# Layer 0 of a hybrid decoder step in two token groups, with one group's conv, norm and attention issued between the other group's dense blocks

## The chip, the cores and the metric

The kernel is one program on one core of a Trainium2 chip. The metric is the device time of one execution in microseconds, as the median over runs. The profile names the engines PE (TensorE matmul), PEld (its weight loads), DVE (VectorE), ACT (ScalarE), POOL (GpSimd) and SP (SyncE, which issues nearly all DMAs). All of them run their own instruction streams in program order and wait for each other through semaphores.

## The reference, cut to what matters

One inference step of a two-layer trunk for 1024 prompt tokens and 64 sample tokens (8 sequences of 8), `D_MODEL` 1024, in float32. Layer 0 is this; layer 1 has another mixer and is not touched in substance.

```python
hn = rms_norm(h, norm_mix_g[0])
a_val, a_gate, q, k, v = split(hn @ w_in)             # 5 x 512 columns
a = causal_depthwise_conv(concat([conv_prev, a_val * sigmoid(a_gate)]), conv_w) + conv_b   # 31 taps, 512 channels
a = silu(layer_norm(a, ln_g, ln_b))
# stick-breaking attention, 8 heads x 64, strictly causal; the sample group has 1024 cached keys in pages besides
z = q @ k.T * scale + bias
after = reverse_cumsum(log_sigmoid(-z)) - log_sigmoid(-z)
b = exp(log_sigmoid(z) + after) @ v
h = h + concat([a, b]) @ w_out
h = h + (silu(g) * u) @ w_ffn_out                     # g, u = split(rms_norm(h) @ w_ffn_in), 2816 each
```

## The kernel before, in words

Activations lie transposed, channels on the partitions and all `T` = 1088 tokens along the free dimension: `hb` holds eight chunks of 128 channels. A dense product is made of column blocks. `mm3` multiplies one 128x128 weight block with the tokens three times (high part by high, high by low, low by high part, for float32 accuracy out of the fast `float32r` type), in three PSUM banks of 364, 364 and 360 tokens: 9 matmuls for a weight block, 72 for a "half".

A half is 128 output columns over 8 input chunks (or 2 input chunks by 512 output columns), 512 KB of weights. `w_load` fetches it through SP into `stage`, `w_split` makes the high part on ACT (line 132) and the low part on POOL (line 133). `w_next` runs this a few halves ahead. The layer-0 stream is 20 halves for the input projection, 8 for the output projection and 66 for the channel mixer; layer 1 has 16, 8 and 66. Every half is fetched and split once, for all 1088 tokens.

The order of the work is written out in program order (`manual_schedule`), one stage after another:

- Start: x is loaded and transposed, its norm made; the input projection begins. DVE evacuates each block from PSUM, times the norm (`scaled`, line 200).
- Conv (`conv_ops`): beside the input projection, by a list of work pieces that `bg(9.0)` takes from after each block. DVE does 21 of the 31 taps of a chunk as multiply-adds from SBUF to SBUF (line 491, one instruction for the prompt and one for the sample tokens). ACT and POOL do 10 taps of the first three chunks (lines 498 and 500).
- Sample attention, with the conv branch's layer norm in between: cached keys are transposed on PE (line 770) and split, scores (797), chances multiplied up by a scan on DVE, weights transposed, values multiplied (877, 886). No dense block runs here.
- Prompt attention, 8 heads x 8 blocks of 128 queries, in four pipelined steps `s1` to `s4`: scores (1069) and their sigmoids on ACT, the mask on POOL (1083), the reverse scan and a product on DVE (1084, 1086), the transposed weights (1106, `ring`), the values (1118, 256 queries at once). The next head's operands are made piece by piece on DVE and POOL (1018, 1020). Only at its end do the first products of the output projection appear.
- Output projection (`run_out`) and channel mixer (`run_ffn`): ACT takes the Silu, POOL multiplies gate by value (325), ACT and DVE split the hidden block (155, 156). Its last two halves (`to_mixer`) also make the operands of layer 1: squares on ACT and POOL, low parts on DVE (line 266).

Layer 1 follows with its own mixer and channel mixer; at the end the output rows are transposed and stored.

Of the kernel before, what the change touches and what calls it, by code (L numbers as in the profile page):

```python
# [27 lines left out]
EXT = CW - 1 + SEQ          # prompt part of the conv rows  # L28
SCW = 8 + CW - 1            # rows of one sample sequence
# [6 lines left out]
# the sums of a column block: two banks at once, then the third  # L36
def parts(acc, *flat):
    yield (acc[:, 0:2, :NW],) + tuple(f[:, 0:2 * NW].rearrange("p (b n) -> p b n", b=2) for f in flat)
    yield (acc[:, 2, :T - 2 * NW],) + tuple(f[:, 2 * NW:T] for f in flat)


@with_exitstack
def trunk_kernel(ctx, tc, x_prompt, x_sample, cache_k, cache_v, state_conformer, state_shortconv, state_pool,
# [8 lines left out]
    tmps = ctx.enter_context(tc.tile_pool(name="tmps", bufs=3))  # L52
# [3 lines left out]

    def tmp():
        return tmps.tile([128, 1152], F, name="tmp")

# [39 lines left out]
    # blocks of the even projection: value 0, gate 1, q 2, k 3, v 4  # L99
    EVEN = [(j, c) for c in range(4) for j in (0, 1, 2, 3)] + [(4, c) for c in range(4)]  # L100
    for j, c in EVEN:
        add_in(w_in_even[0], 512 * j + c * 128)
    for n in range(8):
        add_in(w_out_even[0], n * 128)
    add_ffn(0)
    # blocks of the odd projection: gb 0, gc 1, xv 2, u 3
# [9 lines left out]
    wlim = [len(EVEN)]                # halves that may be fetched so far  # L116

    def w_load(upto):
        while nxt[0] < min(upto, wlim[0]):
            i = nxt[0]  # L120
            src, kt = seq[i]
            stage[i] = wpool.tile([128, 1024], F, name="stage", bufs=4)
            sp.dma_start(stage[i].rearrange("p (k n) -> p k n", k=kt), src)
            nxt[0] += 1

    def w_split(upto):
        while nxt[1] < min(upto, wlim[0]):
# [11 lines left out]
    def w_next(live=0):               # live: halves before this one whose products are not issued yet  # L139
        j = wj[0]  # L140
        wj[0] += 1
        w_split(j + 3 - live)
        w_load(j + 7 - live)
        return hls.pop(j)

# [1 line left out]
    def mm3(acc, wh, wl, x, first, last):  # L147
        for s, (w, xi) in enumerate(((wh, 0), (wh, 1), (wl, 0))):
            for b, (c0, c1) in enumerate(BLOCKS):
                pe.matmul(acc[:, b, :c1 - c0], w, x[:, xi, c0:c1],  # L150
                          start=first and s == 0, stop=last and s == 2)
# [9 lines left out]
    def add_squares(src, first):  # L161
        if first:
            act.activation(ss[:, :T], src, AF.Square)
            return
        t = tmp()
        act.activation(t[:, :T], src, AF.Square)  # L166
        pool.tensor_tensor(ss[:, :T], ss[:, :T], t[:, :T], op=OP.add)  # L167
# [11 lines left out]
        # one Newton step behind the table's square root  # L179
# [5 lines left out]
    def norm_a(ps, count):  # L185
        norm_cols(ps, count, 0, 9)
        dg = tmp()
        dve.tensor_tensor(dg.rearrange("p (t n) -> p t n", t=9), ident[:, None, :].to_broadcast([128, 9, 128]),
                          rstd[:, :, None].to_broadcast([128, 9, 128]), op=OP.mult)
        return dg  # L190

    def norm_b(ps, dg):
        for c0, c1 in ((0, 512), (512, 1024), (1024, T)):
            m = ps()
            pe.matmul(m[:, :c1 - c0], ones, dg[:, c0:c1], start=True, stop=True)
            act.activation(rr[:, c0:c1], m[:, :c1 - c0], AF.Copy)

    def scaled(dst, acc):
        for a, d, r in parts(acc, dst, rr):
            dve.tensor_tensor(d, a, r, op=OP.mult)  # L200

    def added(dst, acc):
        for a, d in parts(acc, dst):
# [12 lines left out]
    def block(a, h, x, ks=K0, mid=None):  # L216
        for i, k in enumerate(ks):
            if i == 4 and mid:
                mid()
            mm3(a, h[:, 0, k], h[:, 1, k], x[k], k == ks[0], k == ks[-1])  # L220

    # two column blocks at once, over the k blocks as they come
    def pair_open(accs):
        return (accs(), w_next()), (accs(), w_next(1))

    def pair_k(st, x, ks, k):
        for a, h in st:
            mm3(a, h[:, 0, k], h[:, 1, k], x[k], k == ks[0], k == ks[-1])

    def pair(accs, x, ks, hooks, st=None, done=0):  # L230
        st = st or pair_open(accs)
        for k in ks[done:]:
            pair_k(st, x, ks, k)
# [4 lines left out]
    def run_in(accs, x, evacs, hooks, bg=lambda us: None, ks=K0, tail=(lambda: None,) * 2):  # L238
        a0, a1 = pair(accs, x, K0, hooks)
        evacs[0](a0)  # L240
        evacs[1](a1)
        bg(14.0)
        for i, e in enumerate(evacs[2:]):
# [3 lines left out]
            block(a, h, x, ks if end else K0, flush)  # L247
# [5 lines left out]
            bg(9.0)  # L253
# [4 lines left out]
    def low(n=0):                     # low parts held back so that they do not stand before the next sums  # L258
# [3 lines left out]
    def prep(x, n, g, squares=False):  # L262
        act.activation(x[n][:, 0], hb[:, n], AF.Copy, scale=g)  # L263
        if squares:
            add_squares(hb[:, n], n == 0)
# [1159 lines left out]
```

## Time and profile before

| | |
|---|---|
| median of 3 runs | 2767.51 us (2767.29 to 2769.02) |
| span of the profiled execution | 2767.4 us |
| PE busy | 2593.5 us, 94% of the span |
| DVE busy | 1186.8 us, 43% |
| POOL busy | 981.4 us, 35% |
| ACT busy | 726.7 us, 26% |
| DMA | 171.96 MB, mean 62 GB/s |

The table's busy shares are means over stages that differ much. A busy instruction of DVE or POOL can include time in which it stands still, so a group's mean duration is to be held against the same instruction elsewhere in the trace. The profiled execution's span is its time from the first to the last instruction; its own time is not listed apart, and the span differs from the median of the runs by 0.1 us.

### The profile page before, as it was taken

To read this page: it belongs to the slowest core of one execution; us is meant where nothing else is said; L and a number is where in the kernel's file an instruction comes from. 1 tells how busy PE (TensorE), PEld (TensorE's weight loads), DVE (VectorE), ACT (ScalarE), POOL (GpSimd) and SP (SyncE) were. 2 spreads that over 40 slices of the span, in tenths; PEclk is the share of its full clock that TensorE was granted. 3 is DMA by queue.
4 is the path that set the end of the run, shared out by engine and by line. 5 is a ranking of instruction groups with operands and counts; after the bars stand their busy time and mean duration, and the time that the engine had idled before them with its cause. 6 is when DMAs were issued, how large, how long until landed. Compare 5 with 4: busy or idle time off the path is not lost.

```text
span 2767.4 us, 35971 instructions
## 1 busy us (share of the span) xinstructions
PE 2593.5 (94%) x15167; PEld 2470.7 (89%) x15167; DVE 1186.8 (43%) x1455; ACT 726.7 (26%) x1038; POOL 981.4 (35%) x497
## 2 busy tenths in 40 slices
PE   7967988777899999999999999999999999999997
PEld 7967955455699999999999999999999999999997
DVE  5889876688623222222222263342322222222226
ACT  4332165566522111111111132122211111111112
POOL 5666223387543222222222242224322222222222
PEclk9988999899999999999999999999999999999999
DMA  6111265212211111111111131131111111111101
GB/s 206 34 41 41 76 229 190 61 39 62 79 46 46 44 41 46 46 46 39 46 46 46 40 112 47 39 106 46 46 47 39 46 47 46 39 46 46 46 31 65
DMA packets 201096, 171.96 MB, mean 62 GB/s; under 512 B 7121, under 2 KB 164945, under 8 KB 200472
## 3 DMA queue, kind: packets, MB, share of 16 engines
q1 hardware_dynamic: 200904, 169.66, 19.6%
q8 instruction: 120, 1.97, 0.3%
q14 instruction: 40, 0.33, 0.0%
q10 hardware_dynamic: 32, 0.01, 0.0%
HBM read 147.76 MB, written 18.69 MB: 60 GB/s over the span
## 4 chain that ended last, share of the span: by engine, by line
PE 81%; DVE 11%; POOL 4%; ACT 2%; issue 1%; DMA 0%; POOLq 0%; DVEq 0%; ACTq 0%; SPq 0%
PE acc L150 74%; DVE hb L491 5%; POOL be L1083 1%; POOL qq L1020 1%; PE o L877 1%; POOL kk L1020 1%; DVE be L1086 1%; PE kts L770 1%; DVE x L266 1%; PE z L797 1%; PE blk L1337 1%; PE o L1118 1%; DVE kth L774 1%; PE m L1106 0%; PE m L415 0%
## 5 line engine op out<-in xcount | busy, mean ns | idle before, releaser
L150 PE MATMUL acc<-x,hl 128*128 128x364 f32 (+1 forms) x10080 | 1706.5, 331 | 24.4 <-DVE tmp L200 17.1
L150 PEld LDWEIGHTS acc<-x,hl 128*128 128x128 f32 x10080 | 1688.9, 189 | 29.8 <-DVE tmp L200 17.3
L133 POOL TENSOR_TENSOR hl<-stage,hl 128x1024 fp32r<-128x1024 f32 x181 | 440.1, 2434 | 1292.4 <-ACT hl L132 825.4
L150 PE MATMUL acc<-hid,hl 128*128 128x364 f32 x3024 | 507.7, 329 | 0.9 <-DVE hb L204 0.9
L150 PEld LDWEIGHTS acc<-hid,hl 128*128 128x128 f32 x3024 | 504.1, 188 | 1.6 <-PE acc L150 1.4
L200 DVE TENSOR_TENSOR tmp<-acc,rr 128x728 f32<-128x728 f32 x228 | 154.4, 719 | 806.6 <-PE acc L150 800.2
L204 DVE TENSOR_TENSOR hb<-acc,hb 128x728 f32<-128x728 f32 x368 | 249.3, 719 | 352.8 <-PE acc L150 352.3
L132 ACT ACTIVATE hl<-stage 128x1024 fp32r<-128x1024 f32 x181 | 190.1, 1054 | 747.5 <-issue 384.9
L491 DVE SCALAR_TENSOR_TENSOR hb<-ext,par,hb 128x1024 f32<-128x1024 f32 (+1 forms) x180 | 208.9, 1232 | 0.0
L312 ACT ACTIVATE tmp<-tmp 128x1088 f32<-128x1088 f32 x44 | 49.0, 1113 | 367.9 <-DVE tmp L200 367.9
L167 POOL TENSOR_TENSOR ss<-ss,tmp 128x1088 f32<-128x1088 f32 x31 | 92.9, 2998 | 129.8 <-ACT tmp L166 129.1
L325 POOL TENSOR_TENSOR tmp<-tmp 128x1088 f32<-128x1088 f32 x44 | 111.5, 2535 | 38.3 <-ACT tmp L312 38.3
L156 DVE TENSOR_TENSOR hid<-tmp,hid 128x1088 fp32r<-128x1088 f32 x44 | 56.9, 1292 | 139.6 <-ACT hid L155 139.6
L155 ACT ACTIVATE hid<-tmp 128x1088 fp32r<-128x1088 f32 x44 | 49.1, 1116 | 216.6 <-POOL tmp L325 216.6
L1084 DVE TENSOR_TENSOR_SCAN q<-q,ss 128x1024 f32<-128x1024 f32 (+3 forms) x64 | 105.0, 1640 | 1.7 <-ACT q L1074 1.4
L1106 PE MATMUL m<-ident,be 128*128 128x128 f32 x288 | 48.0, 298 | 54.4 <-DVE be L1086 51.5
L500 POOL TENSOR_TENSOR hb<-hb,tapb 128x1088 f32<-128x1088 f32 x27 | 89.0, 3295 | 25.2 <-ACT tapb L498 23.9
L1106 PEld LDWEIGHTS m<-ident,be 128*128 128x128 f32 x288 | 33.9, 150 | 70.3 <-issue 51.5
L266 DVE SCALAR_TENSOR_TENSOR x<-hb,par,x 128x1088 fp32r<-128x1088 f32 x32 | 71.2, 2233 | 25.0 <-ACT x L263 25.0
L1086 DVE TENSOR_TENSOR be<-be,q 128x1023 f32<-128x1023 f32 (+3 forms) x64 | 58.0, 906 | 34.6 <-POOL be L1083 32.5
L1118 PE MATMUL o<-ring,tmp 128*64 128x256 f32 (+1 forms) x320 | 71.6, 372 | 0.0
L1118 PEld LDWEIGHTS o<-ring,tmp 128*64 128x64 f32 x320 | 42.4, 141 | 28.9 <-issue 8.8
(236 smaller groups left out, 1572.9 us busy)
## 6 DMA issues: line engine op xcount, KB each, us to landing
stage<-in_w_ffn_in_dram SPq DMA_DIRECT2D x88, 512.0 KB
stage<-in_w_ffn_out_dram SPq DMA_DIRECT2D x44, 512.0 KB
stage<-in_cache_k_dram SPq DMA_DIRECT2D x64, 256.0 KB
stage<-in_w_in_even_dram SPq DMA_DIRECT2D x20, 512.0 KB
vst<-in_cache_v_dram SPq DMA_DIRECT2D x40, 256.0 KB
park<-hb SPq DMA_DIRECT2D x16, 544.0 KB
hb<-park SPq DMA_DIRECT2D x16, 544.0 KB
stage<-in_w_in_odd_dram SPq DMA_DIRECT2D x16, 512.0 KB
```

What stands on the lines that cost most here:

```text
L132: act.activation(hl[:, 0], st, AF.Copy)
L133: pool.tensor_tensor(hl[:, 1], st, f32(hl[:, 0]), op=OP.subtract)
L150: pe.matmul(acc[:, b, :c1 - c0], w, x[:, xi, c0:c1], start=first and s == 0, stop=last and s == 2)
L167: pool.tensor_tensor(ss[:, :T], ss[:, :T], t[:, :T], op=OP.add)
L200: dve.tensor_tensor(d, a, r, op=OP.mult)
L204: dve.tensor_tensor(d, a, d, op=OP.add)
L266: lowq.append(lambda: dve.scalar_tensor_tensor(x[n][:, 1], hb[:, n], g, f32(x[n][:, 0]), op0=OP.mult, op1=OP.subtract))
L325: pool.tensor_tensor(t[:, :T], t[:, :T], u[:, :T], op=OP.mult)
L491: dve.scalar_tensor_tensor(o, i, w, o, op0=OP.mult, op1=OP.add)
L500: pool.tensor_tensor(a2[:, :T], a2[:, :T], t[:, :T], op=OP.add)
L1084: dve.tensor_tensor_scan(q[:, :n][:, ::-1], q[:, :n][:, ::-1], late[:, 1024 - n:][:, ::-1], 1.0, op0=OP.mult, op1=OP.max)
L1118: pe.matmul(o[:, c:], vrow[hp][:, j, hh], ring[:, (b + j) % RING, c:], start=j == 0, stop=j == nk - 1)
```

## The change

Layer 0's tokens are cut into two groups: GA has tokens 0 to 511, GB tokens 512 to 1087 (512 prompt and 64 sample tokens). `Grp` gives each its column blocks: GA one bank of 512 columns, GB two of 288; layer 1 keeps 364/364/360 (`GT`). The dense stages of layer 0 run per group: input projection GA, input projection GB, output projection and channel mixer GA, the same for GB. The weight stream therefore holds every layer-0 half twice: 94 more fetches and splits.

Everything else of layer 0 becomes a generator that issues a piece and yields a cost in us. After a dense block, `bg(us)` runs pieces worth that many us. While the last blocks of GA's input projection (from its block 12) and GB's input projection run, the pieces are GA's conv, layer norm and attention; while GA's output projection and channel mixer run, they are GB's conv, layer norm and attention and then the whole sample attention. Nothing is issued between the blocks of GB's channel mixer but the squares of GA for the next norm.

The taps keep their split between engines, now for all four chunks (10 taps on ACT and POOL, 21 on DVE) and for 512 or 512+64 tokens at a time. The prompt attention works on 128 queries at a time throughout; its scan is cut in two (the masked 128 columns, then the rest). The sample attention makes all its value products in full float32, with two value slots in place of eleven. GA's channel mixer takes the sigmoid on ACT and one more product on POOL in place of the Silu. Stage buffers go from 4 to 3.

```diff
-NW = 364           # token block of one PSUM bank; the third has 360
-BLOCKS = [(0, NW), (NW, 2 * NW), (2 * NW, T)]
+GA = Grp(0, HALF, 512)
+GB = Grp(HALF, T, 288)
+GT = Grp(0, T, 364)
...
+    for _ in range(2):
+        for j, c in EVEN:
+            add_in(w_in_even[0], 512 * j + c * 128)
+    for _ in range(2):
+        for n in range(8):
+            add_in(w_out_even[0], n * 128)
+        add_ffn(0)
...
+    def bg(us):
+        owed[0] = min(owed[0] + us, us + 4.0)
+        while flow and owed[0] > 0:
+            try:
+                cost = next(flow[0])
+            except StopIteration:
+                flow.pop(0)
+                continue
+            if cost is None:
+                return
+            owed[0] -= cost
...
+            if sig:
+                s = tmp()
+                act.activation(s[:, :n], t[:, :n], AF.Sigmoid)
+                pool.tensor_tensor(t[:, :n], t[:, :n], s[:, :n], op=OP.mult)
...
+                for j in range(OFF, CW):
+                    w = pc(CONVW + j * 4 + c)
+                    for o, i in io(a, g.c0, j):
...
+                            dve.scalar_tensor_tensor(o, i, w, o, op0=OP.mult, op1=OP.add)
+                    if j % 2 and j // 2 - OFF // 2 < OFF:
+                        otap(j // 2 - OFF // 2)
+                    yield 0.8 if g is GA else 1.07
...
+            for u in range(len(units) + 3):          # attention(g): 8 heads x 4 query blocks
+                if u >= 3:
+                    s4(u - 3)
+                if 2 <= u < len(units) + 2:
+                    s3(u - 2)
+                if 1 <= u < len(units) + 1:
+                    s2(u - 1)
...
+                    s1(u)
+                for _ in range(2):
+                    if small:
+                        small.pop(0)()
+                yield 1.7 if g is GA else 3.6
...
+    def slot_a(i):
...
+        bg(3.2)
+    in_proj(GA, x1a, 2, slot_a)
...
+    def slot_b(i):
+        bg(7.3)
+    in_proj(GB, x1, 0, slot_b)
+    drain()
...
+    def flow_c():
+        yield from conv(GB)
+        yield from conv_norm(GB)
+        yield from attention(GB)
+        kstack.close()
+        yield from sample()
...
+    def slot_c():
+        bg(6.9)
+    run_out(GA, accs, x1, FFNG, slot=slot_c)
...
+    run_ffn(GA, accs, ms, hidp, x1, last_a, sig=True, slot=slot_c)
...
+    run_out(GB, accs, x1, FFNG)
...
+        run_ffn(GB, accs, ms, hidp, x1, to_mixer, slot=slot_d)
```

POOL in the conv. Before, beside the input projection: L133 makes the low part of a weight half, L500 adds a tap, L577 is the gate product.

```order
L577 TENSOR_TENSOR tmp<-tmp 128x1088
L582 MEMSET ext 128x30
L133 TENSOR_TENSOR hl<-stage,hl 128x1024
L500 TENSOR_TENSOR hb<-hb,tapb 128x1088 x2
L133 TENSOR_TENSOR hl<-stage,hl 128x1024
L500 TENSOR_TENSOR hb<-hb,tapb 128x1088 x3
```

Now, POOL in GB's conv beside GA's channel mixer: L153 is the weight half, L670 the tap, L363 and L377 are the two products of the hidden blocks.

```order
L153 TENSOR_TENSOR hl<-stage,hl 128x1024
L377 TENSOR_TENSOR tmp<-tmp 128x512
L363 TENSOR_TENSOR tmp<-tmp 128x512
L670 TENSOR_TENSOR a_4162<-a_4162,tapb 128x576 x3
L153 TENSOR_TENSOR hl<-stage,hl 128x1024
L670 TENSOR_TENSOR a_4162<-a_4162,tapb 128x576 x2
L153 TENSOR_TENSOR hl<-stage,hl 128x1024
L377 TENSOR_TENSOR tmp<-tmp 128x512
L670 TENSOR_TENSOR a_4358<-a_4358,tapb 128x576 x2
```

Between two weight halves still stand two or three taps, but a half is now used for 512 tokens, so POOL gets them in half the dense time, with the hidden blocks' products besides.

PE in the prompt attention. Before: L1106 transposes weights, L1069 makes scores, L1118 multiplies the values, with nothing else around them.

```order
L1106 MATMUL m<-ident,be 128x128 x8
L1069 MATMUL z_5095<-kk,qq 128x256 x2
L1118 MATMUL o_5107<-ring,tmp 64x256 x3
L1118 MATMUL o_5107<-ring,tmp 64x128
L1106 MATMUL m<-ident,be 128x128 x7
L1069 MATMUL z_5124<-kk,qq 128x384 x4
```

Now, GB's attention (L797 values, L788 transposes, L760 scores) and the block of GA's channel mixer that follows (L170, acc).

```order
L788 MATMUL m<-ident,be 128x128 x7
L760 MATMUL z_6334<-kt,qa 128x320
L760 MATMUL z_6334<-kt,qz_4851 128x320
L760 MATMUL z_6334<-kt,qa 128x320
L760 MATMUL z_6334<-kt,qz_4851 128x320
L797 MATMUL o_6343<-wt,vrow 64x128 x7
L788 MATMUL m<-ident,be 128x128 x6
L760 MATMUL z_6367<-kt,qa 128x512
L760 MATMUL z_6367<-kt,qz_4852 128x512
L760 MATMUL z_6367<-kt,qa 128x512
L760 MATMUL z_6367<-kt,qz_4852 128x512
L170 MATMUL acc<-hid,hl 128x512 x24
```

One or two steps of the attention, each of values, transposes and scores, now stand between two dense blocks of 24 matmuls; the transposes of the second step need the product that DVE makes after the first was issued.

More of the change, by code (lines that the diff above doesn't have):

```diff
@@ L142, in w_next, with mm3 @@
         w_split(j + 3 - live)
-        w_load(j + 7 - live)
+        w_load(j + 6 - live)
         return hls.pop(j)
-    def mm3(acc, wh, wl, x, first, last):
+    def mm3(g, acc, wh, wl, x, first, last):
         for s, (w, xi) in enumerate(((wh, 0), (wh, 1), (wl, 0))):
-            for b, (c0, c1) in enumerate(BLOCKS):
+            for b, (c0, c1) in enumerate(g.blocks):
                 pe.matmul(acc[:, b, :c1 - c0], w, x[:, xi, c0:c1],
@@ new lines, in trunk_kernel @@
+    feed(GA, x1a, 0)
+    w_split(2)
+    feed(GA, x1a, 1)
+    feed(GA, x1a, 2)
+    hooks = {c - 3: [lambda c=c: feed(GA, x1a, c)] for c in range(3, KC)}
+    hooks[5] = [rest]
+    a0, a1 = pair(GA, accs, x1a, K0, hooks)
+    raw = [tmp(), tmp()]
+    for a, o in parts(GA, a0, raw[0]):
+        act.activation(o, a, AF.Copy)
+    for a, o in parts(GA, a1, raw[1]):
+        dve.tensor_copy(o, a)
+    for hf in range(2):
+        for t in range(4, 9):
+            load_x(hf, t)
+    attention_constants()
@@ L539, in trunk_kernel @@
[L539 to L556 removed]
+    glu_done = set()
```

1429 lines of the change are left out of this document (663 added, 766 removed).

## The prediction

> **What bounds the kernel now.** I first cut the span into its stages and read every engine's busy time in each. The columns after the stretch are the busy us of PE, PEld, DVE, ACT and POOL, then the granted clock, the DMA share and GB/s.
>
> ```profile
> core 0: us, PE busy (x) PEld busy (x) DVE busy (x) ACT busy (x) POOL busy (x), PEclk, DMA share, GB/s
> 0.00:60.00 60.00, 45.29 (x265) 41.75 (x265) 33.45 (x37) 30.84 (x34) 37.10 (x21) 0.97 0.69 229
> 60.00:340.00 280.00, 234.03 (x1350) 228.99 (x1349) 248.40 (x236) 76.64 (x120) 137.64 (x52) 0.91 0.15 45
> 340.00:528.00 188.00, 154.74 (x740) 99.55 (x740) 123.82 (x215) 102.74 (x223) 56.50 (x26) 0.94 0.54 178
> 528.00:744.00 216.00, 156.33 (x810) 109.87 (x810) 172.16 (x147) 135.70 (x256) 160.94 (x142) 0.92 0.19 47
> 744.00:1610.00 866.00, 865.60 (x5190) 863.35 (x5191) 230.76 (x305) 149.39 (x143) 245.43 (x100) 1.00 0.15 48
> 1610.00:1671.00 61.00, 57.96 (x333) 55.34 (x332) 38.29 (x39) 27.35 (x29) 34.38 (x13) 0.97 0.31 111
> 1671.00:2767.40 1096.40, 1079.49 (x6485) 1071.89 (x6483) 339.96 (x478) 204.04 (x235) 309.39 (x145) 1.00 0.16 49
> ```
>
> From 744 on PE is full. Ahead of it lie start, input projection with conv, sample attention and prompt attention; PE is not full there, and this is what the change wants to fill. So I looked at what bounds the conv stage: the groups by shape in its window 84 to 258 (five DVE and POOL groups, one evacuation), and behind the dots the same kinds of instruction over the whole trace.
>
> ```profile
> L491 DVE SCALAR_TENSOR_TENSOR hb<-ext,par,hb 128x1024 f32<-128x1024 f32 x53 | 87.0, 1642 | 0.0
> L491 DVE SCALAR_TENSOR_TENSOR hb<-ext,par,hb 128x64 f32<-128x64 f32 x52 | 70.6, 1358 | 0.0
> L200 DVE TENSOR_TENSOR tmp<-acc,rr 128x728 f32<-128x728 f32 x4 | 3.6, 904 | 0.0
> L500 POOL TENSOR_TENSOR hb<-hb,tapb 128x1088 f32<-128x1088 f32 x27 | 89.0, 3295 | 25.2 <-ACT tapb L498 23.9
> L133 POOL TENSOR_TENSOR hl<-stage,hl 128x1024 fp32r<-128x1024 f32 x10 | 25.7, 2573 | 0.0
> ...
> L1247 DVE SCALAR_TENSOR_TENSOR hb<-ext,par,hb 128x1024 f32<-128x1024 f32 x8 | 10.2, 1280 | 0.0
> L1247 DVE SCALAR_TENSOR_TENSOR hb<-ext,par,hb 128x64 f32<-128x64 f32 x8 | 2.2, 280 | 0.0
> L1224 POOL TENSOR_TENSOR tmp<-tmp 128x1088 f32<-128x1088 f32 x4 | 10.1, 2531 | 0.0
> L133 POOL TENSOR_TENSOR hl<-stage,hl 128x1024 fp32r<-128x1024 f32 x181 | 440.1, 2434 | 1292.4 <-ACT hl L132 825.4 <-issue 451.2 <-DMA xt<-in_x_prompt_dram 15.8
> L200 DVE TENSOR_TENSOR tmp<-acc,rr 128x728 f32<-128x728 f32 x114 | 104.4, 915 | 806.6 <-PE acc L150 800.2 <-issue 6.1
> L156 DVE TENSOR_TENSOR hid<-tmp,hid 128x1088 fp32r<-128x1088 f32 x44 | 56.9, 1292 | 139.6 <-ACT hid L155 139.6
> ```
>
> The 64-wide tap takes 1358 ns in the conv and 280 in layer 1, the POOL add 3295 against 2531. The evacuation, whose one input is PSUM, takes 904 and 915: it is not slowed. So DVE instructions with both inputs in SBUF and POOL's tensor operations wait for each other, a whole instruction at a time. At their undisturbed durations the work is 53x1.28 + 52x0.28 + 27x2.53 + 10x2.43 + 2x2.53 (gate products) = 180 us, in a window of 174: DVE and POOL together act as one resource, filled 1.03 times over. I call it the pair.
>
> The prompt attention shows the same at the level of single instructions (scan, POOL low part, POOL mask, product, then a scan of 128 and a product of 127).
>
> ```profile
> 578.91 2.29 DVE L1084 TENSOR_TENSOR_SCAN q<-q,ss 128x1024 f32<-128x1024 f32 x1
> 579.02 2.71 POOL L1020 TENSOR_TENSOR kk<-kall,kk 64x256 fp32r<-64x256 f32 x1 [2.93 <-ACT be L1074]
> 581.81 0.45 POOL L1083 TENSOR_TENSOR be<-be,tri 128x128 f32<-128x128 f32 x1
> 582.30 1.22 DVE L1086 TENSOR_TENSOR be<-be,q 128x1023 f32<-128x1023 f32 x1 [1.09 <-POOL be L1083]
> ...
> 565.08 0.41 DVE L1084 TENSOR_TENSOR_SCAN q<-q,ss 128x128 f32<-128x128 f32 x1
> 592.27 0.29 DVE L1086 TENSOR_TENSOR be<-be,q 128x127 f32<-128x127 f32 x1 [1.08 <-POOL be L1083]
> PE m L1106 <- DVE be L1086: 51.5, 38, 3.1
> ```
>
> The low part stands 2.71 us, 2.2 of them behind the scan; then mask; then product: one after the other. The last line is the wait that costs PE most: transposes behind the product, 51.5 us in 38 times.
>
> The Trainium skill says the same in "SBUF — State Buffer", "Who interferes with whom": a VectorE instruction with two SBUF inputs and a GpSimd instruction that reads SBUF exclude each other for the whole instruction, one SBUF input does not contend. The trace agrees (1358 against 280 ns, 904 against 915). By the rule taken strictly nothing overlaps, and the two conv sections below would be 10 us longer; I keep the measured 1.03.
>
> **The change part by part.** Prices of the pair, on straight lines through those rows: POOL 0.17 + 2.17 ns a column (0.45 at 128, 2.53 at 1088), so 1.28 us at 512 and 1.42 at 576; a weight half 2.4; a tap 0.75 at 512 and 0.28 for the sample tokens; a DVE tensor operation 0.69 at 512, 0.76 at 576; a scan 0.41 at 128, then 0.27 for each further 128.
>
> PE's prices come from steady pieces of the chain (a piece, its us, its count):
>
> ```profile
> 866.16 753.11 PE acc L150 x4518
> 2721.59 1.06 PE blk L1337 x6
> 404.99 0.48 PE z L797 x4
> 553.38 2.52 PE o L1118 x12
> 2721.26 0.33 PE m L1354 x3
> ```
>
> Per column these are 0.460 ns (363 wide), 0.460 (384) and 0.455 (264): proportional, no floor seen, so 512 costs 0.235 us and 288 costs 0.132. A half takes 24x0.235 = 5.64 us for GA and 48x0.132 = 6.34 for GB, together 11.98, as 72x0.1667 = 12.0 before. *Dense PE time does not change.* A float32 value product of 256 columns takes two passes of 0.21 us, a transpose 0.11. What changes is who works beside it, and how often weights are split: 94 more halves x 2.4 = 226 us more for the pair, all in layer 0. The second fetch is 94x0.5 MB; the sample stage with 33.5 MB of pages moved 178 GB/s, GA needs 0.52 MB per 5.64 us = 93: hidden.
>
> Section by section (counts of the instructions as they now stand), pair against PE; the longer sets the time:
>
> - Start and first 12 halves of GA. Before, the first products came at 20 us after nine token tiles; now four, I take 15. Then 12x5.64 + 10 of transposes and norm, and 8 for the norm's chain: 101.
> - GA's conv, 15 halves. A chunk: 20 taps x0.75 + 9 adds x1.28 + 0.7 = 27.2; four 109. Weights 36, gate products 5, first sums of the norm 4: pair 154. PE 95. 154/1.03 = 150.
> - GA's norm, 4 halves: PE 27, pair 30, in a chain: 35.
> - GA's attention, 9 halves. A head: masks 4x0.45, scans 3.7, products 2.0, two low parts 2.6: 10.0; eight 80, weights 22, rest of the norm 5: 107. PE 57 + 40 = 97. Both near full, and a step's transposes wait for its product: I add 10 per cent: 118.
> - GB's conv, 19 halves of GA's output projection and mixer. A chunk: 20x(0.75+0.28) + 9x1.42 + 0.8 = 34.2; four 137. Weights 46, squares 9, low parts 6, hidden blocks 12: pair 210 against PE 110. 210/1.03 = 204. *This is the worst place:* a half of 5.64 us waits for about 11 of the pair.
> - GB's norm, 5 halves: pair 43, PE 30: 45.
> - GB's attention, 18 halves. A head: masks 1.8, scans 8.1, products 4.1, low parts 3.8: 17.8; eight 143. Weights 43, hidden blocks 20: 206. PE 18x5.64 + 89 = 191. With 5 per cent for waits: 216.
> - Sample, 30 halves: PE 169 + 130 (72 value products of 0.84 = 60, 292 transposes 32, scores 30, rest 8) = 299; the pair has 123. Transposes turn over in two PSUM buffers; 0.3 us for 48 steps: 314.
> - Last two halves: 12.
> - GB's output projection and mixer: 72x6.34 = 457 + 10 for change of buffers and the norm: 467. The pair has 243 there and nothing to do besides.
>
> To here: 101 + 150 + 35 + 118 + 204 + 45 + 216 + 314 + 12 + 467 = 1662. Before, this point, the start of the mixer's last two halves, was at 1610:
>
> ```profile
> 1599.76 28.58 PE L150 MATMUL acc<-hid,hl 128*128 128x364 f32 x170
> 1664.66 3.04 PE acc L150 x18
> ```
>
> The first row is PE's last long run in layer 0; its last 108 products (18 us) belong to those halves, the other 36 come singly behind it. The second is the end of the next pair of blocks, at 1667.7: 57 us, in which DVE and POOL held PE up. Now the two halves are 11.3 us shorter on PE and the squares smaller: 46. The rest, 1100 us, stays. 1662 + 46 + 1100 = 2808. The overlaps at the seams (up to three evacuation buffers let PE run on into the next section) I put at 8: **2800 us**. The profiled execution's span is 2767.4, the median 2767.5, so nothing has to be added.
>
> What hides the added splits in GB's mixer is PE (243 against 458 us). In GA's sections that cover is gone, which is where the loss arises; the saving is the empty PE time of the old conv and attention stages (46 us of 280, 33 of 188 and 60 of 216 by the busy rows, more at full pace), and the two nearly cancel.
>
> **Rivals.**
> *PE sets the pace everywhere* (faster). If queued work of the pair were caught up in the next section, or the two engines overlapped, the sections would take PE's 101 + 95 + 30 + 97 + 110 + 35 + 191 + 314 + 12 = 985, and the total 2598. For it: over all sections the pair has 948 us and PE 936, so perfect smoothing would nearly do it. Against it: evacuations stand in DVE's order behind the taps, so PE can lead by three blocks only, and the conv rows above. It decides from 38 us below my sum (2762): with no waits in the attentions (-21), seams counted twice (-8) and an overlap of 1.06 (-10). 0.20.
> *Waits inside the steps* (slower still). PE issues in order, so a transposition that waits now holds a dense block. At 1.36 us (51.5/38) for each of 67 attention steps in place of the 21 us above: +70, 2870. For it: the longest wait row; against it: the product is issued a step earlier. 0.12.
> *Sample values late.* Two value slots instead of eleven: if each of 32 page pairs waits 2 us, +64, 2864. For it: the 178 GB/s of that stage; against it: 49 MB in 314 us are 156. 0.08.
>
> **How the numbers follow.** No change I call within 0.2% of 2767.5, about what runs of this kernel can tell. My case 0.54 (2773 to 2850), its edge with no change 0.06, PE's pace 0.20, the two slower rivals 0.20. Faster 0.20, same 0.06, slower 0.74. Range 2735 (no seams lost, waits all hidden) to 2870.
>
> **What the profile will show.** Dense matmuls at the same pace in GB's mixer, PE full there. In GB's conv PE busy about half, taps far above 0.75 us, POOL adds above 1.42. In the sample section PE near full. Layer 1 unchanged to 10 us. It is wrong if GB's conv section takes near 110 us, or if GB's attention or the sample section exceed PE's time by over 30.

## The result, and the profile after

The changed kernel takes 2956.1 us (median of four runs, 2954.9 to 2957.1) against 2767.4 (four runs, 2767.3 to 2769.0): 1.068 times as long, interval 1.0666 to 1.0696. The direction was forecast, the size was not: +189 us instead of +33, outside the range.

The profiled execution has a span of 2955.4 us. Cut at the borders of the forecast's sections, every engine's busy time reads like this (columns as in the prediction's first view):

```profile
core 0: us, PE busy (x) PEld busy (x) DVE busy (x) ACT busy (x) POOL busy (x), PEclk, DMA share, GB/s
0.00:101.00 101.00, 85.62 (x358) 65.30 (x359) 34.76 (x69) 40.82 (x58) 56.52 (x40) 0.97 0.56 170
101.00:243.00 142.00, 109.03 (x597) 95.55 (x595) 129.58 (x109) 53.92 (x78) 102.63 (x57) 0.88 0.27 77
243.00:298.00 55.00, 40.17 (x252) 37.76 (x252) 15.71 (x21) 16.21 (x23) 36.73 (x24) 0.77 0.15 44
298.00:446.00 148.00, 114.67 (x726) 96.36 (x725) 77.50 (x122) 63.98 (x150) 67.19 (x64) 0.90 0.20 54
446.00:661.00 215.00, 130.66 (x502) 100.32 (x500) 175.57 (x211) 81.24 (x152) 126.20 (x67) 0.79 0.21 61
661.00:731.00 70.00, 43.12 (x164) 33.14 (x162) 27.83 (x38) 19.42 (x28) 48.97 (x31) 0.76 0.15 42
731.00:985.00 254.00, 213.62 (x1169) 174.67 (x1168) 162.87 (x163) 120.19 (x191) 138.16 (x92) 0.92 0.17 47
985.00:1329.00 344.00, 315.66 (x1385) 215.90 (x1384) 132.71 (x258) 116.78 (x239) 95.95 (x52) 0.98 0.49 143
1329.00:1343.00 14.00, 11.07 (x47) 8.29 (x45) 13.84 (x16) 5.95 (x9) 5.13 (x3) 1.00 0.79 261
1343.00:1810.00 467.00, 465.13 (x3504) 464.21 (x3505) 127.06 (x172) 123.95 (x148) 223.88 (x109) 1.00 0.29 86
1810.00:1856.00 46.00, 39.54 (x232) 37.87 (x230) 23.39 (x25) 18.56 (x23) 21.85 (x11) 0.89 0.30 100
1856.00:2955.40 1099.40, 1082.45 (x6504) 1074.55 (x6502) 341.49 (x481) 206.25 (x238) 312.54 (x146) 1.00 0.16 50
```

Row by row against the forecast: start 101 (101), GA's conv 142 (150), its norm 55 (35), its attention 148 (118), GB's conv 215 (204), norm 70 (45), attention 254 (216), sample 344 (314), last halves 14 (12); then GB's output projection and mixer 467 (467), the pair of blocks behind it 46 (46), the rest 1099.4 (1100). From GB's projection on, where TensorE is nearly full, everything was forecast to a microsecond. The 101 us of the first row are the forecast's own border and not a measurement: the twelfth half ends at 106.5 us in the trace, and the first tap of GA's conv starts at 115.9, behind the thirteenth half. The miss is +148 us in the interleaved sections: the two convs together have +3, the norms +45, the attentions +68, the sample section +30. The +3 hangs on the border: here TensorE's wait for the norm's sums (9.9 and 17.1 us) counts to the norm; counted to the conv, as in the table of the experiments, GB's conv takes 231.

In GB's conv (stretch 461 to 655) the groups are those foreseen: the 64-wide tap at 885 ns, the POOL add at 1789 where the prediction's straight line gives 1420.

```profile
L678 DVE SCALAR_TENSOR_TENSOR hb<-ext,par,hb 128x512 f32<-128x512 f32 x69 | 78.0, 1130 | 0.0
L678 DVE SCALAR_TENSOR_TENSOR hb<-ext,par,hb 128x64 f32<-128x64 f32 x68 | 60.2, 885 | 0.0
L670 POOL TENSOR_TENSOR a<-a,tapb 128x576 f32<-128x576 f32 x32 | 57.3, 1789 | 9.4 <-ACT tapb L668 6.4 <-issue 1.5
```

TensorE's waits in all interleaved sections, longest first (waiting matmul, releaser, total us, times, longest):

```profile
PE m L656 <- DMA stc<-in_state_conformer_dram: 56.6, 4, 22.3
PE m L788 <- DVE be L778: 30.3, 19, 4.6
PE m L218 <- POOL ss L689: 27.0, 2, 17.1
PE acc L170 <- DVE hb L230: 21.3, 5, 10.2
PE z L760 <- POOL kt L740: 15.6, 2, 9.1
PE acc L170 <- POOL hl L153: 11.7, 4, 4.7
```

The first is a load of conv states that I had not foreseen. The second (transposes behind the product) and third (the norm's matmul of ones behind GpSimd's sums) are waits of a *step* (one round of the norm or the attention) while dense work stands behind it in TensorE's order.

### The profile page after: what moved, and what is told of

The parts are those of the page before. It is cut to its first block, busy times and chain, and to the rows that moved or that the text cites. A ratio compares the mean times of both kernels' runs of the same rounds, so it can differ in the third digit from the quotient of the medians.

```text
span 2955.4 us, 37943 instructions
## 1 busy us (share of the span) xinstructions
PE 2650.7 (90%) x15423; PEld 2403.9 (81%) x15423; DVE 1262.3 (43%) x1679; ACT 867.3 (29%) x1334; POOL 1235.8 (42%) x688
## 5 line engine op out<-in xcount | busy, mean ns | idle before, releaser
L153 POOL TENSOR_TENSOR hl<-stage,hl 128x1024 fp32r<-128x1024 f32 x278 | 679.2, 2445 | 1265.3 <-ACT hl L152 899.4
L170 PE MATMUL acc<-x1t,hl 128*128 128x364 f32 (+1 forms) x4896 | 825.0, 330 | 7.1 <-DVE hb L230 6.5
L170 PEld LDWEIGHTS acc<-x1t,hl 128*128 128x128 f32 x4896 | 818.1, 190 | 9.2 <-ACT x1t L304 6.7
L170 PE MATMUL acc<-x,hl 128*128 128x288 f32 (+1 forms) x4704 | 790.9, 329 | 25.0 <-POOL hl L153 8.8
L170 PEld LDWEIGHTS acc<-x,hl 128*128 128x128 f32 x4704 | 713.8, 193 | 96.1 <-issue 13.6
L170 PE MATMUL acc<-hid,hl 128*128 128x364 f32 (+2 forms) x3024 | 518.8, 331 | 21.3 <-DVE hb L230 21.3
L170 PEld LDWEIGHTS acc<-hid,hl 128*128 128x128 f32 x3024 | 482.7, 190 | 54.4 <-DVE hb L230 24.4
L226 DVE TENSOR_TENSOR tmp<-acc,rr 128x728 f32<-128x728 f32 (+2 forms) x230 | 160.7, 721 | 792.0 <-PE acc L170 786.8
L230 DVE TENSOR_TENSOR hb<-acc,hb 128x728 f32<-128x728 f32 (+2 forms) x368 | 255.6, 720 | 325.3 <-PE acc L170 324.2
L678 DVE SCALAR_TENSOR_TENSOR hb<-ext,par,hb 128x512 f32<-128x512 f32 x240 | 265.9, 1155 | 2.4
L170 PE MATMUL acc<-x1a,hl 128*128 128x512 f32 x480 | 126.8, 420 | 8.3 <-POOL hl L153 7.1
L670 POOL TENSOR_TENSOR a<-a,tapb 128x512 f32<-128x512 f32 (+1 forms) x72 | 123.3, 1712 | 19.4 <-ACT tapb L668 14.5
L377 POOL TENSOR_TENSOR tmp<-tmp 128x512 f32<-128x512 f32 (+2 forms) x66 | 117.1, 1774 | 28.0 <-ACT tmp L365 28.0
L170 PEld LDWEIGHTS acc<-x1a,hl 128*128 128x128 f32 x480 | 93.6, 199 | 33.5 <-POOL hl L153 8.9
L797 PE MATMUL o<-wt,vrow 128*64 128x128 f32 x576 | 79.9, 286 | 10.1 <-ACT wt L789 9.7
L797 PEld LDWEIGHTS o<-wt,vrow 128*64 128x64 f32 x576 | 64.0, 141 | 29.2 <-ACT wt L789 20.9
L788 PE MATMUL m<-ident,be 128*128 128x128 f32 x288 | 50.3, 308 | 30.3 <-DVE be L778 30.3
```

The lines of the kernel that those rows point to most:

```text
L153: pool.tensor_tensor(hl[:, 1], st, f32(hl[:, 0]), op=OP.subtract)
L170: pe.matmul(acc[:, b, :c1 - c0], w, x[:, xi, c0:c1], start=first and s == 0, stop=last and s == 2)
L230: dve.tensor_tensor(d, a, d, op=OP.add)
L377: pool.tensor_tensor(t[:, :n], t[:, :n], u[:, :n], op=OP.mult)
L670: pool.tensor_tensor(a2, a2, t, op=OP.add)
L678: dve.scalar_tensor_tensor(o, i, w, o, op0=OP.mult, op1=OP.add)
```

## The experiments

To compare sections I read their borders from TensorE's timeline: the first matmul of the norm's sums, the first scores, the first 512-wide block of GA's output projection, the first page transpose, the first 288-wide block of GB's output projection. A wait ahead of such a matmul here counts to the section before it, so the changed kernel's row differs a little from the windows above. GA's conv is counted from 101 us in every row. All columns but the last two are spans in us; then the time at which GB's projection begins, and the device time. Dense halves move a little from section to section; the two columns at the right do not care. e10, b1, b2 and b3 are medians of four runs (the runs of one kernel lie up to 7 us apart), the others single runs.

| kernel | GA conv | norm | attention | GB conv | norm | attention | sample, last | GB projection begins | total |
|---|---|---|---|---|---|---|---|---|---|
| changed | 152 | 55 | 140 | 231 | 59 | 255 | 350 | 1343 | 2956.1 |
| e1 states early | 151 | 55 | 142 | 232 | 60 | 255 | 351 | 1345 | 2959.4 |
| e2 no low parts | 126 | 49 | 143 | 193 | 53 | 234 | 347 | 1246 | 2858.3 |
| e4 norm apart | 152 | 51 | 127 | 231 | 74 | 238 | 334 | 1307 | 2919.9 |
| e6 half slots | 154 | 48 | 129 | 230 | 57 | 240 | 329 | 1288 | 2901.5 |
| e7 = e4 + e6 | 154 | 48 | 122 | 232 | 70 | 225 | 314 | 1266 | 2878.2 |
| e5 all DVE | 146 | 47 | 135 | 213 | 54 | 235 | 352 | 1283 | 2896.7 |
| e10 = e7 + e5 | 146 | 45 | 118 | 205 | 64 | 212 | 317 | 1207 | 2823.7 |
| e9 = e7 + e2 | 126 | 43 | 110 | 194 | 59 | 214 | 313 | 1162 | 2773.9 |
| e11 = e9, one tap | 101 | 42 | 110 | 138 | 57 | 214 | 313 | 1075 | 2688.9 |

### Is the longest wait on the path? (e1)

```
 with tc.tile_pool(name=f"conv{g.c0}", bufs=1) as ep:
+    for c in range(4 if g is GB else 0):
+        stcs.append(ep.tile([128, 2, 128], F, name="stc", bufs=4))
+        ...                                    # both loads, as before
...
-        stc = ep.tile([128, 2, 128], F, name="stc")
+        stc = stcs[c]
```

> The changed kernel with the conv states of all four channel chunks of the second group loaded when its conv begins, instead of each with its chunk. In the changed kernel TensorE waits 56.6 us in this section for the state's loads (22.3, 14.4 and 19.5 us at one time). Theory A (the pair of VectorE and GpSimd sets the conv's time, the wait only lies beside it): GB conv stays at 215 us within 10, the total at 2946 to 2956; TensorE waits there for something else. Theory B (the late load is on the path): GB conv falls by about 50, the total to about 2905.

Measured 2959.4: nothing gained. TensorE's waits in that conv (446 to 662) show why:

```profile
PE acc L170 <- DVE hb L230: 23.5, 4, 11.8
PE acc L170 <- POOL hl L153: 19.3, 9, 3.6
PE acc L170 <- DVE tmp L226: 17.4, 2, 12.6
PE acc L170 <- ACT hl L152: 14.2, 4, 6.5
PE m L659 <- DMA stc<-in_state_conformer_dram: 1.5, 1, 1.5
```

The state's wait fell from 56.6 to 1.5 us, and the waits for evacuations (lines 230, 226) and weight splits (153, 152) rose from 26.0 to 74.4. So the load was not what held the conv; that the pair holds it (VectorE's two-input instructions and GpSimd's, which take turns) is what e2 and e11 show. The wait that TensorE's list put first had a cover. A long wait row is a place, not a price.

### Whose work sets which section? (e2)

```
+            if i < 114:
+                hls[i] = High(hl[:, 0]...)     # index for low part gives the high part
+                nxt[1] += 1
+                continue
             pool.tensor_tensor(hl[:, 1], st, f32(hl[:, 0]), op=OP.subtract)
```

> The changed kernel without GpSimd's low parts of the weights for the first 114 halves (all up to GB's output projection): the third product of each matmul triple takes the high part once more, so TensorE, ScalarE and the loads do what they did, and the output lacks the weights' low parts there. GpSimd loses 114 x 2.4 = 274 us of work. Theory A (the pair's work sets the time of all interleaved sections): GA conv 142 to about 115, GA norm 55 to 40, GA attention 148 to 125, GB conv 215 to 168, GB norm 70 to 55, GB attention 254 to 220, sample 344 to 335; total about 2790. Theory B (in the norms, the attentions and the sample section TensorE's own work and its waits for the steps of the other group set the time; the pair only in the two convs): GA conv and GB conv fall as above, the norms by 5 to 10 each, the attentions and the sample by no more than 10 each; total about 2855.

Measured 2858.3, what Theory B gave (2855). The convs lose 25.5 and 37.7 us of the 36 and 46 that their splits cost uncontended, both norms 6, GB's attention 21, GA's nothing. GB's attention lost twice what Theory B allowed it (10), and less than Theory A's 34: the pair has a part there too. In GA's attention (3 us longer) and the sample section (4 us shorter) this run shows no part of it.

### TensorE's waits inside the steps (e4, e6, e7)

The norms' matmuls one dense block later, in three places of this kind:

```
-        yield 4.0
+        yield 4.0 + (3.2 if g is GA else 6.9)
         spread(g, ms, ss[:, cs], 1.0 / 512)
```

> The changed kernel with one more dense block between each matmul of the two conv norms and the GpSimd or VectorE work that it waits for (three places in each norm). In the changed kernel TensorE waits there 27.0 us for the sums and 12.9 us for the diagonals. Theory A (the pair is behind with its work and sets the norms' time): the waits move to the dense blocks' evacuations and the total stays within 8 of 2956. Theory B (TensorE, issuing in order, waits inside the norm while dense work stands behind): the two norm sections, taken with as many dense blocks as they held before, lose 25 to 35 us together; total 2920 to 2930.

Measured 2919.9, as Theory B had it (36 us). Half of it came in GA's part (output projection begins at 430 instead of 448), half in GB's. But it did not come where Theory B had put it. The norms now hold 6 and 8 dense halves instead of 5 and 6; less those halves (5.64 us each) they are 10 us shorter in GA's part and 3 longer in GB's. GB's attention, with 18 halves before and after, is 17 us shorter: TensorE is idle there for 30 us instead of 39, and its own work takes 208 instead of 216 us, at a granted clock of 0.97 instead of 0.92.

Pieces in the middle of each block as well, half as much at each place:

```
-            block(g, a, h, x)
+            block(g, a, h, x, mid=half)
...
     def slot_c():
-        bg(6.9)
+        bg(3.45)
...
-run_ffn(GA, accs, ms, hidp, x1, last_a, sig=True, slot=slot_c)
+run_ffn(GA, accs, ms, hidp, x1, last_a, sig=True, slot=slot_c, half=slot_c)
```

> The changed kernel with the pieces of the other group's work issued at twice as many places, half as much at each: also in the middle of every dense block, so that in GB's attention one step stands between two half blocks instead of two steps in a row between two blocks. Theory A (the pair sets the time): total within 15 of 2956, the waits for the products only change their place. Theory B (waits inside the steps): in GA's attention TensorE waits 33 us, in GB's 40 us, mostly since the second of two steps turns the product that the first has only just issued; half of it goes: GA attention about 133, GB attention 232, sample 335, conv 205; total 2890 to 2915.

Measured 2901.5, again Theory B (54.6 us): 15 us in GB's attention, 10 in GA's, 22 in the sample section, none in the convs, where it had foreseen 10. The reason I gave lies in the order of a step: the product of tile u-1 is issued in one step, its transposes in the next, and with two steps in a row between blocks every second transposition comes only a step's few microseconds after its product. The waits bear it out only in part. In GA's attention the transposes' wait fell from 14.9 to 10.1 us; in GB's it did not fall with this edit, only with both (the changed kernel in 738 to 993, e6 in 720 to 960, e7 in 727 to 952):

```profile
PE m L788 <- DVE be L778: 15.4, 7, 4.6
...
PE m L790 <- DVE be L780: 16.7, 11, 3.5
...
PE m L790 <- DVE be L780: 6.6, 6, 2.6
```

What e6 gained in GB's attention lies in other waits (an evacuation, 7.0 us, and those for the attention's copies and operands, 8 us together) and in the clock, 0.96 instead of 0.92. That smaller pieces in more places give 55 us is shown; through which wait, in part.

> The changed kernel with both edits of the first four runs that took TensorE's waits inside the steps away: pieces also in the middle of each block, and the norm's matmuls a place later. Alone they gave 36 and 54 us. If the waits are separate ones (norm against attention and sample) the total is about 2868; if both gave the same thing back (later dense work, the clock), about 2895.

Both together: 2878.2, 78 us, 13 less than the sum; so mostly separate waits. Between 101 us and GB's projection TensorE's idle time falls from 264 to 204 us and its busy time from 978 to 961. The two rows that the edits were made for account for 26 us of that, the transposes' wait down from 30.3 to 18.8, the norms' sums from 27.0 to 12.3; the rest is many shorter ones:

```profile
PE m L790 <- DVE be L780: 18.8, 15, 2.6
PE m L218 <- POOL ss L691: 12.3, 2, 8.4
```

### What did interleaving hide at all? (e3)

```
 flow.append(flow_c())
 owed[0] = 0.0
+drain()
 mix_operand(GA, x1, K0)
```

> The changed kernel with the second group's conv, norm and attention and the sample attention issued in one go ahead of the first group's output projection and mixer, so that nothing is interleaved in that part; then 88 dense halves with TensorE full, 88 x 5.64 = 496 us. In the changed kernel the four steps and these halves take 895 us together. Theory A (interleaving hides what the pair's price sum says): alone the conv takes 142, the norm 40, the attention 155, the sample 190: 527 + 496 + 8 = 1031, total about 3090; interleaving hides 136 of the 496. Theory B (waits inside the steps eat the gain): the steps alone are quicker than that, since no dense block stands between them (conv 137, norm 30, attention 140, sample 175), and the total comes to 3040 or less.

That text has a slip: 74 halves run there (8 of the output projection, 66 of the mixer), not 88; 74 x 5.64 = 417 us, Theory A's total becomes 527 + 417 + 8 = 952 for the part, 3013 in all, and Theory B's 2968. Measured 3002.5, between the two and nearer to A. Conv, norm, attention, sample and then the dense halves stand one after the other, cut by the table's borders:

```profile
448.00:572.30 124.30, 3.03 (x8) 1.33 (x8) 118.28 (x172) 42.40 (x98) 71.41 (x39) 0.51 0.02 7
572.30:608.20 35.90, 7.05 (x18) 4.55 (x18) 8.95 (x15) 10.46 (x15) 24.34 (x19) 0.50 0.07 14
608.20:760.30 152.10, 115.28 (x752) 95.07 (x753) 129.21 (x118) 94.72 (x162) 74.50 (x58) 0.90 0.06 14
760.30:957.90 197.60, 167.30 (x693) 92.29 (x693) 79.65 (x184) 78.11 (x189) 0.00 (x0) 0.91 0.59 169
957.90:1389.00 431.10, 422.12 (x1788) 334.58 (x1787) 132.86 (x195) 125.11 (x153) 244.39 (x126) 1.00 0.34 102
```

The steps alone take 124 + 36 + 152 + 198 = 510 us. Undoing the interleaving of the whole part costs only 46 us (3002.5 - 2956.1) of the 417 it could have hidden, and 14 of these are the dense halves' own (431 for 417). GB's attention is the clearest: alone 152; in the changed kernel 255 with 18 halves beside it, which by themselves take 102. Subtracted, 153 us are left: interleaving hid nothing. In e7 the same sum (18.5 halves) leaves 120, in e9 110.

### Less work for the pair, in both kernels (e5, e10, b1, b2, b3)

VectorE instead of GpSimd for weights' low parts, taps, masks and attention's low parts:

```
-            pool.tensor_tensor(hl[:, 1], st, f32(hl[:, 0]), op=OP.subtract)
+            (dve if i < 114 else pool).tensor_tensor(hl[:, 1], st, f32(hl[:, 0]), op=OP.subtract)
...
-    OFF = 10
+    OFF = 0
...
-                pool.tensor_tensor(be[:, n - 128:n], be[:, n - 128:n], tri, op=OP.mult)
+                dve.tensor_tensor(be[:, n - 128:n], be[:, n - 128:n], tri, op=OP.mult)
```

> The changed kernel with VectorE in GpSimd's place for the low parts of the first 114 weight halves (about 1.25 us instead of 2.4), for all 31 taps of each conv chunk (no adds on GpSimd, no products on ScalarE) and for the attention's low parts and masks. The pair's price sum falls by 114 x 1.15 = 131 for the weights, 4 x 3.9 + 4 x 2.3 = 25 for the taps and about 35 in the attentions. Theory A (the pair): GA conv 152 to 120, GB conv 231 to 195, the rest together by 60; total about 2830. Theory B (waits inside steps, pair only in the convs): the convs as above, attentions and sample by 15 together; total about 2870. Theory C (two engines beside each other after all): VectorE alone gets longer, conv sections 10 to 30 us longer; total above 2970.

Measured 2896.7, above Theory A and Theory B (2830, 2870) and below the changed kernel by 59 us; in the convs only 6 and 17 us where I expected 32 and 36. I had left VectorE's evacuations out of the sum. They read PSUM and can run beside GpSimd (904 and 915 ns in the kernel before, with GpSimd busy and quiet), but not beside VectorE's own taps: in GA's conv the engine is busy for 128 of 146 us. In GB's it is busy for 175 of 214, so there this explains it only in part. Theory C (VectorE alone takes longer) is wrong.

> The changed kernel with both edits against the waits, and VectorE in GpSimd's place for the low parts of 114 halves, all conv taps and the attention's masks and low parts. Alone they gave 78 and 59 us. Separate causes: about 2820, still slower than before by 2 per cent; one cause: about 2855.

Measured 2823.7 (2820.1 to 2827.3): 132 us, of the 137 that both gains add up to. It is the best version of the grouped kernel, and still 1.020 of the kernel before (interval 1.0184 to 1.0219).

The same edit belongs in the kernel before, whose conv stage is held by the pair too:

```
-    OFF = 10
+    OFF = 0
...
+            (dve if i < 20 else pool).tensor_tensor(hl[:, 1], st, f32(hl[:, 0]), op=OP.subtract)
...
-        def pieces(dst, src, n, eng=pool):
+        def pieces(dst, src, n, eng=dve):
```

and the mask at line 1083 on VectorE.

> The kernel before, not split in groups, with VectorE in GpSimd's place for the low parts of the 20 weight halves of the input projection, all conv taps, and the prompt attention's masks and low parts. By the pair: conv chunk 31 x 1.56 = 48.4 instead of 31.2 + 22.8 + 1.2 = 55 three times (-20), weights 18 x 1.2 (-22), so 30 to 40 us of the projection stage; masks 64 x 0.2 and low parts about 10 in the attention. Total about 2725 to 2740, which beats both kernels. If VectorE and GpSimd do work beside each other, VectorE alone has 28 us more in a stage where it is already at 89 per cent, and the total is 2775 to 2790.

Measured 2714.3 (2712.3 to 2715.4), ratio 0.981, interval 0.9790 to 0.9823: better than both kernels, and 11 us below the range expected. Its conv groups in 84 to 258, and its rows of the conv and attention stages:

```profile
L491 DVE SCALAR_TENSOR_TENSOR hb<-ext,par,hb 128x1024 f32<-128x1024 f32 x92 | 116.9, 1271 | 0.0
L491 DVE SCALAR_TENSOR_TENSOR hb<-ext,par,hb 128x64 f32<-128x64 f32 x91 | 31.5, 346 | 0.0
L133 DVE TENSOR_TENSOR hl<-stage,hl 128x1024 fp32r<-128x1024 f32 x14 | 17.0, 1211 | 7.3 <-ACT hl L132 7.3
...
60.00:340.00 280.00, 254.57 (x1559) 247.97 (x1557) 248.95 (x362) 64.52 (x126) 31.48 (x17) 0.97 0.27 81
528.00:744.00 216.00, 179.79 (x993) 141.31 (x991) 162.21 (x247) 122.56 (x221) 17.05 (x7) 0.97 0.22 63
```

The 64-wide tap falls from 1358 to 346 ns once GpSimd is quiet, the 1024-wide from 1642 to 1271; VectorE does 92 taps in the window instead of 53 at the same busy time (248.95 us against 248.40 in 60 to 340), and TensorE gets 20 us more work done there. This agrees with the rule of the Trainium skill that the prediction quoted ("SBUF — State Buffer", "Who interferes with whom").

> The kernel before with VectorE in GpSimd's place only in the projection stage (20 weight halves, all conv taps). By the pair's sums 30 to 40 us of the 52 that the kernel with both edits gained: 2728 to 2738.

> The kernel before with VectorE in GpSimd's place only for the prompt attention's masks and low parts: the rest of the 52 us, 12 to 22: 2745 to 2755. If the wait of TensorE for the product (51.5 us) is mostly the mask's detour over GpSimd behind the scan, more: 2735.

Measured 2729.9 (2728.3 to 2730.3) and 2752.2 (2751.0 to 2752.3), both inside what was written: 39 and 17 us, together 55 where both edits at once gave 52.5.

### Closing the account (e9, e11)

> The changed kernel with both edits against TensorE's waits inside the steps and without GpSimd's low parts of the first 114 weight halves (the third product takes the high part once more). Alone the two gave 78 and 98 us. If waits and the pair's work are separate causes the total is about 2780; if the half slots and later norms only gave the pair time to catch up (one cause, seen twice) about 2830.

Measured 2773.9, the first theory's 2780: waits and pair are separate causes. GB's attention and the sample section are now nearly at TensorE's pace, idle for 5 and 14 us:

```profile
634.30:848.50 214.20, 208.89 (x1197) 170.84 (x1197) 153.77 (x163) 120.08 (x193) 73.96 (x69) 0.98 0.21 59
848.50:1161.60 313.10, 299.36 (x1329) 204.35 (x1329) 134.57 (x260) 115.22 (x237) 26.34 (x19) 0.99 0.54 159
```

The last kernel leaves 30 of the 31 taps of both convs out as well.

> As the kernel with both edits against the waits and without the weights' low parts, and the two convs reduced to one of 31 taps (no adds on GpSimd, no products on ScalarE); the pace at which pieces are issued is kept. What then stands above the 2598 us of 'TensorE sets the pace everywhere' is TensorE's own price. Theory A (the two convs were the last place of the pair; TensorE's steps cost about 12 us more than forecast in GB's attention, 12 in GA's, 14 in the sample, and each norm's chain 10): GA conv 126 to about 100, GB conv 194 to about 135, total 2670 to 2700. Theory B (a wait of another kind, TensorE issuing in order, still holds GB's conv): GB conv stays above 165, total 2720 or more.

Measured 2688.9, inside Theory A. GB's conv fell from 194 to 138 us (135 foreseen) with 21.5 halves beside it, which by themselves take 121; GA's from 126 to 101 (100 foreseen). TensorE's busy time from 101 to the start of GB's projection:

```profile
101.00:201.00 100.00, 99.50 (x600) 89.13 (x599) 15.38 (x27) 28.12 (x39) 8.67 (x11) 1.00 0.38 107
201.00:1076.50 875.50, 825.40 (x4228) 637.36 (x4227) 431.08 (x656) 384.82 (x706) 222.67 (x200) 0.98 0.36 104
```

## Why the prediction was wrong

Taken apart in this order, the 2956 us are 2689 + 85 (the taps of the convs on all engines, e9 to e11) + 104 (weight splits, e7 to e9) + 78 (TensorE's waits inside the steps, with the slower clock that follows them, changed to e7).

- **Dense PE time unchanged, what follows unchanged: right.** 467, 46 and 1099 us were met; these rows needed a price per column and, for the 46, the 57 us read from the kernel before. The start was 5 us short (twelve halves by 106.5 us for 101).
- **The pair: right in mechanism and in size.** The forecast put 210 us on it and its small allowances (2808 - 2598); without the allowances in attentions and norms (11 + 10 + 5 + 2) it is 182. Taps and splits measured 85 + 104 = 189. That the two convs came within 3 us of their sum is partly luck: GA's 142 for 150 starts at a border that its taps reach 15 us late, and GB's 215 for 204 leaves out the wait in front of the norm. Strict exclusion, the other value that the prediction worked out (154 and 210), fits these two rows as well as 1.03 does.
- **The step that failed: "I add 10 per cent", "with 5 per cent for waits", "0.3 us for 48 steps", and the norms "in a chain".** In those sections I took the longer of two engine sums and added a little. That came within about a tenth where one resource is far ahead, as in the convs. Where TensorE and the pair were nearly equal and handed work to and fro, the time came near to the *sum* of the steps alone and the dense halves: GB's attention 152 + 102 against 255 measured. The allowances were 11 + 10 + 15 us; two small edits against the waits remove 78, and what they don't remove is in the next point.
- **TensorE's own steps were priced too low.** Forecast 95 + 30 + 97 + 110 + 35 + 191 + 299 + 12 = 869 us of TensorE work from 101 to GB's projection. In e11, where little stops it, the same instructions take 925, 56 more; another 35 us of idle time and seams make up the 91 us by which e11 stands above 2598. One half (5.6 us) of the 56 is the late start. Another part is the price in proportion to the columns: 16 matmuls of value products of 128 columns in a row took 1.96 us and 8 transposes in a row 1.03 at the full clock (changed kernel, 756 to 761 us). With the row's start and end that is 0.12 and 0.13 us each, where the prediction's prices give 0.105 (half of the 0.21 for 256 columns) and 0.11. For e11's 576 and 636 of them I estimate 22 us from these rows.
- **The sum of the miss:** 78 (waits) + 91 (dearer steps, idle left) - 21 (the pair, 189 for 210) + 8 (the seams that I subtracted) = 156 = 2956 - 2800.
- **The rivals.** "PE sets the pace everywhere" fell. "Waits inside the steps" named the missing cause and had 0.12; I priced it by one wait row of before (1.36 us a step, attention only), which gave +70. The norms' waits, those of the sample section, and that two steps now stand in a row, weren't in it. "Sample values late" fell: TensorE waited for those loads 2.6 us in the stretch 993 to 1329 and the section ran at 143 GB/s.
- **The forecast's own test spoke:** GB's attention exceeded TensorE's busy time by 40 us (254 against 213.6), the sample section by 28; the limit set was 30.

What stays open: the rest of the 56 us in e11, some 28. Its granted clock of 0.98 over 974 us can hold up to about 19 of them (an estimate from that mean). How the 35 idle us divide among issue gaps and the last waits was not taken apart, nor through which waits e6 gained its 22 us in the sample section.

## What to carry to other kernels

Where two engines are both nearly full in a section (here 191 and 206 of a forecast 216 us) and pass work to each other in program order, don't forecast the longer sum plus a few per cent; forecast the steps' time alone plus the dense blocks, and count an overlap only where producer and consumer are issued well apart. With a block between them in the norms and pieces at twice as many places, GB's attention, less its dense halves, went from 153 to 120 us; alone it takes 152. Before believing a wait row, ask what the engine that it waits beside is doing: the longest one here (56.6 us) was worth nothing, and two edits made against shorter ones (30.3 and 27.0) gave 78 us, more than those rows hold. And where a stage is full of VectorE instructions with two SBUF inputs, sum both engines' work as one before giving GpSimd a part: here VectorE alone was faster.

## What the runs showed of the hardware

The first is that moving a quarter of the taps back *onto* the busier engine pays, which was not foreseen when the prediction was written: VectorE alone took 1271 + 346 ns a tap with GpSimd quiet, against 1642 + 1358 with it helping.

The second is what a stop costs TensorE. In the changed kernel, at the start of GB's attention (the stretches, then single instructions on the timeline):

```profile
739.00:743.00 4.00, 0.03 (x1) 0.03 (x1) 0.00 (x0) 0.00 (x0) 3.77 (x4) 0.50 0.37 109
743.00:747.00 4.00, 1.79 (x4) 0.97 (x5) 1.16 (x2) 2.12 (x2) 1.35 (x2) 0.50 0.08 22
747.00:751.00 4.00, 4.00 (x10) 3.34 (x11) 3.68 (x3) 2.27 (x3) 3.92 (x2) 0.50 0.02 4
751.00:755.00 4.00, 4.00 (x15) 3.18 (x14) 0.71 (x2) 0.58 (x1) 3.29 (x2) 0.78 0.00 0
755.00:759.00 4.00, 3.17 (x22) 2.56 (x21) 2.92 (x4) 2.20 (x5) 1.21 (x2) 1.00 0.77 197
...
737.89 0.79 PE L760 MATMUL z<-kt,qa 128*128 128x512 f32 x1 [6.51 <-POOL kt L740]
742.97 0.79 PE L760 MATMUL z<-kt,qz 128*128 128x512 f32 x1 [4.29 <-POOL qz L743]
748.49 7.70 PE L170 MATMUL acc<-x,hl 128*128 128x512 f32 x24
```

After waits of 6.51 and 4.29 us the granted clock is 0.50, and a half of 24 matmuls takes 7.70 us, not 5.64, until it is back at 1.00. Over all interleaved sections TensorE was busy 978 us in the changed kernel (the rows from 101 to 1343 above) and 925 in e11 for the same matmuls within 0.3 per cent of the records: 53 us of slower running on top of the waits themselves. The granted clock over these sections is 0.89 in the changed kernel and 0.98 in e11. No run changed the clock by itself, so that the clock makes all of the 53 us is argued from the rows and not shown by an experiment. The Trainium skill has this in "TensorE: Matmul & The Clock Gate", section "HAM oscillation — how this bites in real kernels": no idle gaps over about 3.4 us, else the next work starts at half the clock. The rows agree with the half clock after 6.51 and 4.29 us; no run here measures where the limit lies. The prediction had not used it.
